# A one-core hybrid decoder layer: the recurrence's first head beside dense columns, another place for the half steps, and a merge with loads and products ahead

## Chip, cores and metric

One core of one Trainium2 chip. The metric is device microseconds of one execution, the median of 3 runs of the kernel before.

## The reference, cut to what matters

One layer of a decoder on 512 prompt tokens and 8 x 4 sample tokens (544 together), width 1024, all in fp32:

```python
x = layer_norm(ALPHA*x + 0.5*(1 + mod[2]) * swiglu(u0, ...), ln_g[0], ln_b[0])
u = x*(1 + mod[4]) + mod[3]
proj = u @ w_in + b_in            # RWKV columns, queries, keys, values, gates, two merge gates
y_a, new_prev, new_wkv = rwkv7_time_mix(p_rw, rw_prev, rw_wkv, ...)
y_b, new_win = nsa_fn(p_q, sigmoid(p_gate), ...)
m = (sigmoid(p_mA) * (y_a @ w_out_a) + sigmoid(p_mB) * (y_b @ w_out_b)) @ w_o
x = layer_norm(ALPHA*x + (1 + mod[5])*m, ln_g[1], ln_b[1])
x = layer_norm(ALPHA*x + 0.5*(1 + mod[8]) * swiglu(u2, ...), ln_g[2], ln_b[2])
```

`rwkv7_time_mix` is, per head of 64: `S = S*w + (S @ -kk)(kk*a)^T + v k^T`, `y = S @ r`; then a group norm over each head's channels, times `ln_w` plus `ln_b`, plus a bonus term, all times `g = sigmoid(gd) @ g2`. `new_prev` is the last token's row of the projected RWKV columns.

## The kernel before, in words

**Products.** A product in fp32 is done as three (`split`, L254 to L265: ScalarE copies the rounded high part `whi`, VectorE subtracts to get `wlo`; then high by high, high by low, low by high). One column of 128 output channels for 544 tokens (a "dense column") is `dense`, 48 matmuls at L280 with 1024 rows of weights, 24 with 512. A "half step" is `dense_half` (L289), 12 matmuls: half of the tokens of one column of `w_out_b`.

**Order of the work.** A tile scheduler orders each engine's instructions by the program's order and priority. Generators (`yield`) interleave independent work: each `next` issues one step. The stages that matter here:

1. The attention's steps, `prompt_steps` (scores at L1125, transposes L1146, values L1163), with one dense column (`dense_todo`) issued after each step, until 5 columns are left; those after step 31, down to 2 (loop at L1456). The last two are issued by the loop behind the loads of `xwa`, `w2e` and others. These columns are merge gates (`merge_gate`), stored to `gdr` in DRAM.
2. The recurrence. There are four `rw_head`s, each two real heads on 128 partitions. `rw_front` loads r, k and v, and in 7 steps computes decay, key norm and the scaled vectors `be`, `ka`, `ar`, `rk` (products at L1541, L1552, L1570, L1575 and by `head_sums` at L1522; transposes of the sample state at L1603). `rw_prompt` and `rw_sample` then run in turn: chunked products L1630, small inverses in blocks of 32 x 32 (four groups of matmuls, L1690, L1698, L1716, L1724), the chunk chain L1783, and for the sample tokens L1820 to L1893. `rw_tail` does the norm, the bonus, the product with `g2t` (L1522 with `sgd`) and the split into `yah`. The next head starts when the one before has taken 9 steps (`RW_LAG`), with up to 4 live. `wob_steps` holds 16 half steps (8 columns of y_b @ w_out_b, times gate, stored as `mbd`); the main loop issues one in every third round at a raised priority. `ar`'s second half (L1589), `ka` (L1593) and `rk` (L1596) are on GpSimd, the rest of the front on VectorE and ScalarE.
3. The merge. The last-token rows are transposed (L1993) and stored, the residual `xT` is read back whole (L2002), and for each of 8 columns the gate and `mbd` are loaded (L2011, L2012), `w_out_a`'s column is loaded and split (L251 raw), 24 matmuls run at L280, VectorE gates and adds, and `ln_affine` (ScalarE, L194) prepares the residual's tile.
4. The product with `w_o`, the norm and the second feed-forward.

PSUM tiles `mm` have two buffers and `sm` the others. Tags `e` (18 buffers) and `f` (17) hold the head's vectors. All loads named here go through SyncE's queue (SP), in its order.

## Time and profile before

| | us |
|---|---|
| median of 3 runs (1776.05 to 1788.5) | 1780.0 |
| the profiled execution | 1790.0 |
| its span | 1788.2 |
| TensorE busy in it | 1683.7 (94%) |
| mean granted TensorE clock | 0.964 |

The profiled execution is 10 us over the median, of which 1.8 lie outside its span. PE is TensorE's matmuls, PEld its weight loads, DVE is VectorE, ACT ScalarE, POOL GpSimd, SP SyncE. A granted clock of 1.00 is 2.4 GHz and 0.50 is 1.2 GHz. Lines such as L280 are lines of the kernel before.

### The profile page before, as it was taken

The page shows a single profiled execution, that of the slowest core. Times are in us where ns is not written, and L with a number is a line of the kernel's source. Part 1 is how long each engine was busy: PE and PEld are TensorE (multiplying, and loading weights), DVE is VectorE, ACT ScalarE, POOL GpSimd, SP SyncE. Part 2 cuts the span into 40 slices and gives each one's busy share as a digit, 9 for nine tenths or more (in the row PEclk, how much of TensorE's full clock was granted, in tenths as well). Part 3 has the DMA queues.
Part 4 walks back from the last instruction along what each step waited for, and adds up shares of the span by engine and source line. Part 5 has one row for each costly group of instructions (what it writes and reads, how often), then busy time and mean ns, then how long its engine had stood idle before and what let it go on. Part 6 is the DMA issues. An engine that isn't in the chain of part 4 may idle for free.

```text
span 1788.2 us, 34732 instructions
## 1 busy us (share of the span) xinstructions
PE 1683.7 (94%) x14710; PEld 1528.2 (85%) x14710; DVE 883.3 (49%) x1820; ACT 601.9 (34%) x1093; POOL 263.3 (15%) x302
## 2 busy tenths in 40 slices
PE   5999999999999999899999979999899999999995
PEld 5888899999998888677787867877798999999994
DVE  6664233223325735555566376775677333333345
ACT  4343221221224543343444242332446321222221
POOL 6640000000000213445200022231002000000001
PEclk9999999999999999999999988898899999999998
DMA  7853653563534285565432051110642323223321
GB/s 274 298 190 113 200 188 95 189 193 114 159 94 88 94 247 159 172 203 156 122 105 85 32 158 51 46 33 21 219 124 71 95 85 94 83 83 95 92 63 51
DMA packets 260725, 224.97 MB, mean 126 GB/s; under 512 B 28741, under 2 KB 225767, under 8 KB 260186
## 3 DMA queue, kind: packets, MB, share of 16 engines
q1 hardware_dynamic: 244946, 182.60, 34.2%
q0 software_dynamic: 9728, 33.56, 5.8%
q10 hardware_dynamic: 5896, 6.60, 1.1%
q8 instruction: 116, 1.90, 0.4%
q14 instruction: 39, 0.32, 0.1%
HBM read 199.55 MB, written 23.17 MB: 125 GB/s over the span
## 4 chain that ended last, share of the span: by engine, by line
PE 78%; DVE 7%; issue 5%; POOL 3%; DMA 3%; ACT 3%; SPq 0%; another core or an unknown queue 0%; ACTq 0%; POOLq 0%; DVEq 0%
PE mm L280 47%; PE mm L289 8%; PE mm L401 5%; PE sm L520 2%; POOL sraw L1217 2%; PE sm L289 2%; PE sm L1820 1%; PE sm L1630 1%; PE mm L1522 1%; PE sm L1658 1%; PE sm L1163 1%; DMA raw<-in_phi_w1t_dram 1%; PE mm L1125 1%; DMA raw<-in_ffn_w_down_dram 1%; DVE e L174 1%
## 5 line engine op out<-in xcount | busy, mean ns | idle before, releaser
L280 PE MATMUL mm<-uh,whi 128*128 128x272 f32 (+1 forms) x1888 | 398.0, 292 | 2.1 <-ACT qs L194 1.3
L280 PE MATMUL mm<-uh,wlo 128*128 128x272 f32 (+1 forms) x1888 | 393.2, 290 | 0.5 <-DVE wlo L180 0.5
L262 ACT CAST whi<-raw 128x1024 fp32r<-128x1024 f32 (+2 forms) x178 | 177.5, 998 | 642.2 <-PE mm L280 582.3
L280 PE MATMUL mm<-ul,whi 128*128 128x272 f32 (+1 forms) x1888 | 392.5, 289 | 0.0
L180 DVE TENSOR_TENSOR wlo<-raw,whi 128x1024 fp32r<-128x1024 f32 (+2 forms) x178 | 208.2, 1170 | 263.7 <-ACT whi L262 257.3
L280 PEld LDWEIGHTS mm<-uh,whi 128*128 128x128 f32 x1888 | 299.0, 189 | 22.2 <-ACT hh L798 9.2
L280 PEld LDWEIGHTS mm<-ul,whi 128*128 128x128 f32 x1888 | 300.4, 189 | 1.0 <-issue 1.0
L280 PEld LDWEIGHTS mm<-uh,wlo 128*128 128x128 f32 x1888 | 298.0, 189 | 1.8 <-DVE sg L174 0.8
L174 DVE TENSOR_TENSOR sg<-mm,sg 128x544 f32<-128x544 f32 (+1 forms) x47 | 32.3, 688 | 165.4 <-PE mm L280 159.2
L677 POOL TENSOR_TENSOR xT<-xT,mr 128x272 f32<-128x272 f32 x24 | 25.2, 1065 | 557.3 <-DVE xT L174 547.8
L401 PE MATMUL mm<-cx,w1h 128*128 128x256 f32 x512 | 100.3, 291 | 3.7 <-ACT cx L353 1.9
L280 PE MATMUL mm<-hh,whi 128*128 128x256 f32 x480 | 99.3, 288 | 0.0
L280 PE MATMUL mm<-hh,wlo 128*128 128x256 f32 x480 | 99.0, 288 | 0.0
L280 PE MATMUL mm<-hlo,whi 128*128 128x256 f32 x480 | 98.9, 287 | 0.0
L401 PEld LDWEIGHTS mm<-cx,w1h 128*128 128x128 f32 x512 | 82.4, 193 | 11.2 <-issue 6.7
L280 PEld LDWEIGHTS mm<-hh,whi 128*128 128x128 f32 x480 | 76.8, 188 | 1.7 <-ACT hh L798 1.7
L280 PEld LDWEIGHTS mm<-hlo,whi 128*128 128x128 f32 x480 | 76.9, 188 | 0.0
L280 PEld LDWEIGHTS mm<-hh,wlo 128*128 128x128 f32 x480 | 76.8, 188 | 0.0
L401 PE MATMUL mm<-cx,w1l 128*128 128x256 f32 x256 | 73.7, 288 | 0.0
L1217 POOL DMA_INDIRECT sraw<-in_cache_kv_sel_dram,idx x64 | 63.6, 993 | 59.5 <-DMA t_new_kv_win_sample_dram<-sraw 22.6
L732 POOL TENSOR_TENSOR yo<-yo,lno 128x512 f32<-128x512 f32 (+1 forms) x5 | 8.4, 1670 | 396.0 <-issue 372.1
L183 DVE SCALAR_TENSOR_TENSOR xT<-mm,modT,xT 128x512 f32<-128x512 f32 (+2 forms) x80 | 46.4, 582 | 40.5 <-PE mm L289 40.5
(530 smaller groups left out, 3006.8 us busy)
## 6 DMA issues: line engine op xcount, KB each, us to landing
araw<-in_w_ada_dram SPq DMA_DIRECT2D x56, 512.0 KB
raw<-in_ffn_w_gate_dram SPq DMA_DIRECT2D x44, 512.0 KB
raw<-in_ffn_w_up_dram SPq DMA_DIRECT2D x44, 512.0 KB
raw<-in_w_in_dram SPq DMA_DIRECT2D x36, 512.0 KB
raw<-in_ffn_w_down_dram SPq DMA_DIRECT2D x32, 448.0 KB
raw<-in_w_ada_dram SPq DMA_DIRECT2D x16, 512.0 KB
raw<-in_ffn_w_down_dram SPq DMA_DIRECT2D x16, 512.0 KB
gdr<-gst ACTq DMA_DIRECT2D x16, 272.0 KB
```

The source lines that it names most:

```text
L174: V.tensor_tensor(out, a, b, ALU.mult)
L180: V.tensor_tensor(out, a, b, ALU.subtract)
L183: V.scalar_tensor_tensor(out, a, s, b, o0, o1)
L262: S.copy(hv, raw)
L280: T.matmul(ps[:m, h, :n], ww[:, k, :m], xx[:, c0:c0 + n], start=(k == 0 and j == 0), stop=(k == nk - 1 and j == 2))
L289: T.matmul(ps[:, :n], ww[:, k, :], xx[:, c0:c0 + n], start=(k == 0 and j == 0), stop=(k == nk - 1 and j == 2))
L401: T.matmul(pss[:, o, 256 * v:256 * v + 256], ww[:, v, o, jj, :], xx, start=(jj == 0 and j == 0), stop=(jj == 7 and j == 2))
L520: T.matmul(hold["ps"][32 * q:32 * q + 32, :], silT[:, k, :], raws_[i][:, h * 512:(h + 1) * 512], start=(k == 0), stop=(k == KT - 1), tile_ ...
L677: G.tensor_tensor(n, n, mr, ALU.subtract)
L1125: T.matmul(ps[:, g, 0:nk], qT[64 * g:64 * g + 64, i, qt * 128:(qt + 1) * 128], kvt[br, 0][64 * g:64 * g + 64, 0:nk], start=True, stop=True)
L1163: T.matmul(acc[64 * g:64 * g + 64, kt * 128:], kvtok[br][:, kt, 128 + 64 * g:192 + 64 * g], pt_[g][:, 512 * kt:384 * kt + 512], start=(br ...
L1217: G.indirect_dma_start(out=t, out_offset=None, in_=seltab, in_offset=bass.IndirectOffsetOnAxis(ap=idx8[:, c * NB + b:c * NB + b + 1], axis=0))
```

## The change

Six edits go together.

1. Three more dense columns are held back in the attention (8 instead of 5 up to step 31, then 5 instead of 2), and the five left are issued one per step beside the first five of the first head's seven front steps. For this the tags that the front needs (`e`, `ar` and others) move to a pool on the right side that opens earlier, and the last gates take their tiles from tag `e`.
2. `rw_prompt` yields True instead of None after each of its first three stages of 32 x 32 blocks, and a half step is issued there instead of in every third round; what is left runs after the last head.
3. `ar`'s second half and `ka` go from GpSimd to VectorE (`rk` stays).
4. The product with `g2t`, the bonus times it, and the affine weight times it move from `rw_tail` to the end of `rw_sample`; the tail has one product fewer and no GpSimd addition.
5. The transposes and stores of the last-token rows move into two of the `wob_steps` (n = 2 and 3).
6. The merge loads three columns ahead, multiplies the first three of four 128-row pieces of the first two columns before their fourth (which needs the last head), reads `xT` tile by tile after each column, and runs `ln_affine` two columns later, the last two inside the product with `w_o`.

```diff
-        if len(dense_todo) > (5 if n < 31 else 2):
+        if len(dense_todo) > (8 if n < 31 else 5):
...
-    for f in dense_todo:
-        f()
     sta.close()
-    stu.close()
-    stw.close()
-    yap = pool("yap")
...
+    stq.close()
+    strp = ExitStack()
+    rp = pool("rp", stack=strp, side="right")
-    NE, NF = 18, 17
+    NE, NF = 18, 14
...
-        G.tensor_tensor(ar[:, 1, :], wc, xr, ALU.mult)
         mul(ar[:, 0, :], wm1, kk)
         mul(be, kk, ta)
         mul(be, be, wi)
-        G.tensor_tensor(ka, km, wi, ALU.mult)
+        mul(ar[:, 1, :], wc, xr)
+        mul(ka, km, wi)
...
-        yield
+        yield True
...
         mul(v272(bon), halves(ps), v272(xv))
-        d["bon"] = bon
+        yield
+        ps = head_sums(g2t[:, ht * 128:(ht + 1) * 128], sgd)
+        gw = ee()
+        act(v272(gw), halves(ps), AF.Identity, scale=pcol(GNW + ht))
+        stt(v272(bon), v272(bon), pcol(GNB + ht), halves(ps), ALU.add, ALU.mult)
+        d.update(bon=bon, gw=gw)
     def rw_tail(ht, d):
...
-        mul(y, y, r2)
-        yield
-        act(y, y, AF.Identity, bias=pcol(GNB + ht), scale=pcol(GNW + ht))
-        G.tensor_tensor(y, y, d["bon"], ALU.add)
-        ps = head_sums(g2t[:, ht * 128:(ht + 1) * 128], sgd)
-        mul(v272(y), v272(y), halves(ps))
-        S.copy(yah[0][:, ht, :], y)
+        mul(gw, gw, r2)
+        yield
+        add(gw, gw, bon)
+        S.copy(yah[0][:, ht, :], gw)
...
     def wob_steps():
         for n in range(KT):
+            if n in (2, 3):
+                for j4 in (2 * n - 4, 2 * n - 3):
...
+    live = [heads.pop(0)]
+    age = {id(live[0]): 7}
+    for _ in range(7):
+        if dense_todo:
+            dense_todo.pop(0)()
+        next(live[0])
+    stu.close()
+    stw.close()
     while heads or live:
...
-        if k % 3 == 1:
-            with tc.high_priority(offset=-WOB_OFF):
-                next(wst, None)
-        k += 1
+            elif said is True:
+                with tc.high_priority(offset=-WOB_OFF):
+                    next(wst, None)
     for _ in wst:
         pass
...
-    SY.dma_start(xT, xsp)
+    def merge_load(n):
+        raw = load_raw(wview(woa, 0, 512, n * 128, (n + 1) * 128))
+        t = [op.tile([128, TOK], F32, tag=tag, name=f"{tag}{n}", bufs=6) for tag in ("gate", "mb")]
+        SY.dma_start(t[0], gdr[0, n])
+        SY.dma_start(t[1], mbd[n])
+        return raw, t
+    ahead = [merge_load(n) for n in range(3)]
+    parts = []
+    for n in range(2):
+        parts.append((mm(), split(ahead[n][0])))
+        merge_part(*parts[n], 0, 3)
     for n in range(KT):
+        if n + 3 < KT:
+            ahead.append(merge_load(n + 3))
+        if n < 2:
+            merge_part(*parts[n], 3, 4)
...
-        ln_affine(0, n)
+        SY.dma_start(xT[:, n, :], xsp[:, n, :])
+        if n > 1:
+            ln_affine(0, n - 2)
     def out_w(n):
+        if n < 2:
+            ln_affine(0, KT - 2 + n)
```

Where the change moves instructions, first on PE (line, operation, out<-in, shape, count), at the end of the first head's front. Before, the last rows of a half step, then the key-norm product, the second head's first products, the state's transposes and the first L1630:

```order
L289 MATMUL sm_1470_10988<-ybh1_10736,whi_1456_10933 128x272
L289 MATMUL sm_1470_10988<-ybh0_10735,wlo_1457_10934 128x272
L1522 MATMUL mm_1459_10951<-e_1453_10926,cst_r_10756 128x272 x2
L1541 MATMUL mm_1516_11191<-w2e_10749,tw_10758 128x128 x4
L1541 MATMUL mm_1516_11191<-w2e_10749,tw_10758 32x128
L1552 MATMUL mm_1523_11230<-xwa_10748,a2t_10750 128x272 x2
L1603 MATMUL sm_1476_11017<-cst_g_118,sraw_1448_10902 128x64 x8
L1630 MATMUL sm_1486_11036<-ar_1473_11006,e_1471_11004 64x128 x8
L1630 MATMUL sm_1487_11047<-ar_1473_11006,e_1471_11004 64x128 x8
```

After (line numbers are three lower), the last rows of the fifth dense column, then the same transposes, the second head's first products and the first L1627:

```order
L279 MATMUL mm_1462_10891<-uh_163_1486,wlo_1453_10814 128x256
L279 MATMUL mm_1462_10891<-uh_163_1486,wlo_1453_10814 128x288
L1600 MATMUL sm_1470_10965<-cst_g_118,sraw_1431_10655 128x64 x8
L1538 MATMUL mm_1505_11129<-w2e_10569,tw_10578 128x128 x4
L1538 MATMUL mm_1505_11129<-w2e_10569,tw_10578 32x128
L1549 MATMUL mm_1512_11168<-xwa_10568,a2t_10570 128x272 x2
L1627 MATMUL sm_1480_10997<-ar_1467_10954,e_1465_10952 64x128 x8
L1627 MATMUL sm_1481_11008<-ar_1467_10954,e_1465_10952 64x128 x8
```

The dense columns, which stood wholly ahead of the front, now end right in front of the transposes; the half step of that place is gone.

PE again, in the blocks of 32 x 32 of the third head. Before, from the second group of blocks (L1698) to the fourth (L1724):

```order
L1698 MATMUL sm_1787_12755<-x32_1762_12595,w1_1775_12667 32x32 x32
L1639 MATMUL sm_1790_12798<-cst_g_118,e_1672_12115 128x128 x4
L1522 MATMUL mm_1803_12857<-e_1674_12122,brk_1802_12855 128x272
L1893 MATMUL sm_1792_12805<-cst_g_118,f_1683_12168 64x128 x4
L1893 MATMUL sm_1793_12811<-cst_g_118,f_1683_12168 64x128 x4
L1783 MATMUL sm_1798_12829<-f_1748_12528,f_1721_12364 64x64 x2
L1522 MATMUL mm_1803_12857<-e_1674_12122,brk_1802_12855 128x272
L1716 MATMUL sm_1800_12835<-t32_1788_12789,f_1691_12198 32x32 x8
L1603 MATMUL sm_1805_12864<-cst_g_118,sraw_1730_12416 128x64 x8
L1783 MATMUL sm_1807_12875<-f_1748_12528,f_1721_12364 64x64 x2
L1716 MATMUL sm_1800_12835<-t32_1788_12789,f_1691_12198 32x32 x8
L1724 MATMUL sm_1808_12879<-x32_1762_12595,w1_1799_12834 32x32 x8
```

After, from the second group (L1695) on, with the product with `g2t` and the transposes of the sample's state:

```order
L1695 MATMUL sm_1786_12719<-x32_1758_12548,w1_1770_12615 32x32 x32
L1636 MATMUL sm_1789_12762<-cst_g_118,e_1671_12084 128x128 x4
L1519 MATMUL mm_1814_12901<-sgd_10581,g2t_10571 128x272
L1890 MATMUL sm_1791_12769<-cst_g_118,s0T_1683_12153 64x128 x4
L1890 MATMUL sm_1792_12775<-cst_g_118,s0T_1683_12153 64x128
L288 MATMUL sm_1793_12783<-ybh0_10555,whi_1781_12682 128x272
L288 MATMUL sm_1793_12783<-ybh1_10556,whi_1781_12682 128x272
```

A half step (12 rows L288) now stands between the second and the third group of blocks, another inside the third group and one ahead of the second; before, one stood ahead of the second and the next behind the fourth, and the stretch above had none.

Last, SP's queue at the end of the recurrence. Before, the last stores (`mbd6`, the states), the whole `xT`, `mbd7`, and the loads of `w_out_a`:

```order
L1962 DMA mbd6_13375<-gst_1856_13180 128x544
L1896 DMA out_new_wkv_sample_dram<-sraw_1890_13438 64x8x64 x2
L1808 DMA out_new_wkv_prompt_dram<-so_1915_13597 64x2x64
L2002 DMA xT2_13825<-xsp_6101 128x4352
L1962 DMA mbd7_13650<-gst_1902_13511 128x544
L251 DMA raw_1948_13843<-in_w_out_a_dram 128x4x128
L251 DMA raw_1952_13883<-in_w_out_a_dram 128x4x128
```

After:

```order
L1978 DMA mbd6_13786<-gst_1942_13752 128x544
L2063 DMA xT2_13838<-xsp_6101 128x544
L1978 DMA mbd7_13825<-gst_1948_13791 128x544
L2063 DMA xT2_13838<-xsp_6101 128x544 x2
L2031 DMA gate0_13852<-gdr0_0_10389 128x544
L250 DMA raw_1955_13850<-in_w_out_a_dram 128x4x128
L2032 DMA mb0_13853<-mbd0_11410 128x544
```

The loads of `w_out_a` and of the gates now stand behind the store `mbd7`, which waits for the last half step, and behind three tiles of `xT` of 272 KB each instead of the whole one.

## Rows read from the trace of the kernel before

**Rows 1.** The page of the profile, two rows: each engine's busy time with its share of the span and its instructions; and PE's granted clock in 40 slices of 44.7 us, in tenths.

```profile
PE 1683.7 (94%) x14710; PEld 1528.2 (85%) x14710; DVE 883.3 (49%) x1820; ACT 601.9 (34%) x1093; POOL 263.3 (15%) x302
...
PEclk9999999999999999999999988898899999999998
```

**Rows 2.** Busy time by stretch (the columns: start and end, length, busy us and instructions of PE, PEld, DVE, ACT, POOL, then PE's granted clock, the busy share of the DMA engines and their rate). The stretches: the end of the attention with its last dense columns; dense columns and the attention's last step; the first head's front; the recurrence; its end with the first two merge columns; the other six merge columns.

```profile
943.60:991.90 48.30, 46.07 (x279) 31.79 (x278) 28.53 (x71) 21.48 (x59) 0.00 (x0) 0.89 0.20 57
991.90:1027.00 35.10, 35.10 (x275) 33.67 (x274) 9.61 (x15) 9.51 (x19) 0.00 (x0) 1.00 0.11 40
1027.00:1048.50 21.50, 11.77 (x79) 9.44 (x78) 12.62 (x18) 13.04 (x27) 5.83 (x4) 0.82 0.95 260
1048.50:1259.00 210.50, 203.12 (x2942) 162.08 (x2943) 144.61 (x384) 62.81 (x124) 47.96 (x51) 0.88 0.18 51
1258.90:1283.30 24.40, 19.43 (x115) 14.97 (x116) 13.42 (x25) 13.75 (x22) 2.68 (x2) 0.72 0.61 196
1283.30:1301.40 18.10, 18.08 (x144) 18.10 (x145) 17.07 (x25) 7.74 (x13) 0.00 (x0) 1.00 0.77 207
```

**Rows 3.** The same columns for pieces of the first of those stretches.

```profile
968.40:979.20 10.80, 8.77 (x53) 5.04 (x52) 9.72 (x23) 7.37 (x20) 0.00 (x0) 1.00 0.07 26
979.20:989.40 10.20, 10.00 (x26) 4.42 (x28) 6.88 (x22) 3.59 (x15) 0.00 (x0) 0.50 0.00 1
```

**Rows 4.** The waits of PE between 943 and 1030 us (who waited at which line, for whom, us in total, times, longest).

```profile
PE mm L1125 <- ACT pp L194: 2.2, 1, 2.2
```

**Rows 5.** The waits of PE between 1027 and 1049 us.

```profile
PE sm L1630 <- DVE e L174: 9.7, 1, 9.7
```

**Rows 6.** The chain of work that ended last, between 1027 and 1050 us (start, us, what).

```profile
1026.93 0.38 PE mm L280 x3
...
1046.47 1.86 DVE e L174
...
1048.46 1.54 PE sm L1630 x14
```

**Rows 7.** VectorE and GpSimd at the end of that front, as a list of instructions (start, us, engine, line, operation).

```profile
1044.06 0.71 DVE L174 TENSOR_TENSOR e<-e,e 128x544 f32<-128x544 f32 x1
1044.69 1.85 DVE L174 TENSOR_TENSOR ar<-e,e 128x544 f32<-128x544 f32 x1
...
1044.08 1.88 POOL L1589 TENSOR_TENSOR ar<-e,e 128x544 f32<-128x544 f32 x1
```

**Rows 8.** The recurrence, cut where PE's granted clock changes; the columns are those of the second group. Of the seven stretches at half clock these are the first, the second, the fifth and the last.

```profile
1048.50:1054.30 5.80, 5.80 (x58) 5.30 (x59) 5.52 (x12) 0.37 (x1) 1.84 (x3) 0.50 0.76 157
...
1081.60:1098.60 17.00, 15.70 (x160) 13.25 (x159) 6.39 (x14) 4.43 (x9) 3.17 (x7) 0.50 0.17 33
...
1194.20:1201.00 6.80, 6.80 (x66) 6.13 (x62) 3.15 (x6) 0.74 (x2) 0.00 (x0) 0.50 0.00 0
...
1235.20:1238.60 3.40, 3.40 (x29) 2.70 (x24) 0.87 (x2) 1.17 (x2) 1.89 (x5) 0.50 0.02 5
```

**Rows 9.** Three us before that fifth stretch and the first three of it, in the same columns; then the costliest groups of matmuls in the three before (line, operation, shapes, count, busy us, mean ns).

```profile
1191.00:1194.00 3.00, 3.00 (x68) 2.61 (x66) 1.42 (x4) 1.32 (x3) 0.79 (x2) 1.00 0.57 93
1194.00:1197.00 3.00, 3.00 (x44) 2.60 (x43) 0.76 (x2) 0.38 (x1) 0.00 (x0) 0.53 0.00 0
...
L1716 PE MATMUL sm<-t,f 32*32 32x32 f32 x28 | 1.2, 192 | 0.0
L1724 PE MATMUL sm<-x,w 32*32 32x32 f32 x22 | 1.1, 193 | 0.0
```

**Rows 10.** The matmuls of one half step alone, in two places (the columns without the other engines).

```profile
1094.50:1097.80 3.30, 3.09 (x12) 2.77 (x12) 0.50 0.02 5
1110.50:1112.70 2.20, 1.78 (x12) 1.56 (x12) 1.00 0.00 0
```

**Rows 11.** PE's work in the recurrence by line, between 1049 and 1259 us: the half steps.

```profile
L289 PE MATMUL sm<-ybh,whi 128*128 128x272 f32 x112 | 28.2, 348 | 0.0
...
L289 PE MATMUL sm<-ybh,wlo 128*128 128x272 f32 x56 | 18.4, 329 | 0.0
```

**Rows 12.** The same between 1258.9 and 1283.3 us: the product with `g2t` and the transposes of `lastc`.

```profile
L1522 PE MATMUL mm<-sgd,g2t 128*128 128x272 f32 x8 | 3.2, 534 | 0.5 <-DVE e L183 0.5
L1993 PE MATMUL sm<-cst_g,lastc 128*9 128x128 f32 x14 | 2.4, 305 | 1.9 <-ACT so L169 1.9
```

**Rows 13.** The chain of work that ended last, between 1255 and 1312 us.

```profile
1249.86 9.23 DMA xT<-xsp
...
1274.77 8.53 PE mm L280 x48
...
1283.32 18.29 PE mm L280 x144
```

**Rows 14.** ScalarE between 1258.9 and 1275 us: the residual's `ln_affine` and the split's first half.

```profile
L194 ACT ACTIVATE xT<-xT,pv 128x512 f32<-128x512 f32 x8 | 6.3, 807 | 1.3 <-DMA xT<-xsp 1.3
...
L262 ACT CAST whi<-raw 128x512 fp32r<-128x512 f32 x2 | 1.2, 602 | 0.0
```

**Rows 15.** Two stretches of 4 us at the end of the recurrence, in the columns of the second group.

```profile
1250.00:1254.00 4.00, 3.45 (x123) 2.90 (x117) 2.80 (x9) 0.00 (x0) 0.00 (x0) 1.00 0.80 274
1254.00:1258.00 4.00, 3.17 (x75) 2.20 (x67) 1.99 (x7) 2.03 (x3) 0.00 (x0) 1.00 0.93 356
```

**Rows 16.** The DMAs issued between 1236 and 1330 us: the sum of their packets.

```profile
DMA packets 20666, 15.86 MB, mean 169 GB/s; under 512 B 1961, under 2 KB 18345, under 8 KB 20530
```

More of the change, by code (lines that the diff above doesn't have):

```diff
@@ L41 @@
 RW_LAG = 9
-RW_SAMPLE = 0
 AHEAD = 2
@@ L1441, in build @@
     dense_cols = [(j * 128, rw_proj, (j,)) for j in (12, 13, 4, 0, 8, 5, 1, 9, 6, 2, 10, 7, 3, 11)]
-    dense_cols += [(MG0 + s_ * D + n * 128, merge_gate, (s_, n, gsp)) for s_ in (1, 0) for n in range(KT)]
+    dense_cols += [(MG0 + s_ * D + n * 128, merge_gate, (s_, n, lambda: gate_tile[0]()))
+                   for s_ in (1, 0) for n in range(KT)]
+    gate_tile = [lambda: gsp.tile([128, TOK], F32, tag="gst", name=nm("gst"), bufs=3)]
     def dense_step(i):
@@ L1934, in rw_head @@
         a, b = rw_prompt(ht, d), rw_sample(ht, d)
-        live, n = [a, b], 0
+        live = [a, b]
         while live:
+            small = False
             for g_ in list(live):
-                if (g_ is a or n >= RW_SAMPLE) and next(g_, live) is live:
+                said = next(g_, live)
+                if said is live:
                     live.remove(g_)
-            n += 1
-            yield
+                else:
+                    small = small or said is True
+            yield small
         yield from rw_tail(ht, d)
@@ L1946, in wob_steps @@
         for n in range(KT):
+            if n in (2, 3):
+                for j4 in (2 * n - 4, 2 * n - 3):
+                    m = min(4, RW_TILES - 4 * j4)
+                    tps = sm()
+                    for j in range(m):
+                        T.transpose(tps[:9, j * 128:(j + 1) * 128], lastc[:, 4 * j4 + j, :], ident)
+                    so = ff([9, 512])
+                    S.copy(so[:, 0:m * 128], tps[:9, 0:m * 128])
+                    cols = slice(512 * j4, 512 * j4 + m * 128)
+                    SY.dma_start(O["new_shift_prompt"][0:1, 0, cols].rearrange("a b -> a b"), so[0:1, 0:m * 128])
+                    SY.dma_start(O["new_shift_sample"][0, :, cols], so[1:9, 0:m * 128])
             raw = wp.tile([128, wn], F32, tag="raw", name=nm("raw"), bufs=4).rearrange("p (a b) -> p a b", a=4)
@@ L1968, in build @@
     heads = [rw_head(ht) for ht in range(4)]
-    live, age, k = [], {}, 0
+    live = [heads.pop(0)]
[6 more added lines that the diff above has]
+    stw.close()
+    yap = pool("yap")
+    yah = [yap.tile([128, 4, TOK], F32R, name=f"yah{i}") for i in range(2)]
+    str_ = ExitStack()
+    wp, wn = pool("wps", stack=str_), 512
+    rq = pool("rq", stack=str_)
     while heads or live:
@@ L1975, in build @@
             age[id(g_)] += 1
-            if next(g_, heads) is heads:
+            said = next(g_, heads)
+            if said is heads:
                 live.remove(g_)
-        if k % 3 == 1:
-            with tc.high_priority(offset=-WOB_OFF):
-                next(wst, None)
-        k += 1
+            elif said is True:
+                with tc.high_priority(offset=-WOB_OFF):
+                    next(wst, None)
     for _ in wst:
@@ L1984, in build @@
     str_.close()
+    strp.close()
     wp, wn = pool("wp2"), 1024
     sty.close()
[L1987 to L1997 removed]
     xp = pool("xp2", stack=stx, side="right")
     xT = xp.tile([128, KT, TOK], F32, name="xT2")
[L2002 removed]
     up = pool("up2")
@@ L2007, in build, with merge_part @@
     u = new_u()
-    gate, mb = {}, {}
-    for n in range(KT):
-        gate[n], mb[n] = [op.tile([128, TOK], F32, tag=tag, name=f"{tag}{n}", bufs=6) for tag in ("gate", "mb")]
-        SY.dma_start(gate[n], gdr[0, n])
-        SY.dma_start(mb[n], mbd[n])
-        ps = mm()
-        raw = load_raw(wview(woa, 0, 512, n * 128, (n + 1) * 128))
-        dense(ps, split(raw), lambda k: (yah[0][:, k, :], yah[1][:, k, :]), 4)
-        ga = gate[n]
+    def merge_load(n):
[4 more added lines that the diff above has]
+        return raw, t
+    def merge_part(ps, w, k0, k1):
+        hv, lv = w
+        for k in range(k0, k1):
+            for j, (ww, xx) in enumerate(((hv, yah[0]), (hv, yah[1]), (lv, yah[0]))):
+                for h in range(2):
+                    T.matmul(ps[:, h, 0:272], ww[:, k, :], xx[:, k, 272 * h:272 * h + 272],
+                             start=(k == 0 and j == 0), stop=(k == 3 and j == 2))
+    ahead = [merge_load(n) for n in range(3)]
[3 more added lines that the diff above has]
+        merge_part(*parts[n], 0, 3)
+    for n in range(KT):
+        if n + 3 < KT:
+            ahead.append(merge_load(n + 3))
+        if n < 2:
+            ps = parts[n][0]
+            merge_part(*parts[n], 3, 4)
+        else:
+            ps = mm()
+            merge_part(ps, split(ahead[n][0]), 0, 4)
+        ga, mb = ahead[n][1]
         stt(v272(ga), v272(ga), 1.0, halves(ps), ALU.add, ALU.mult)
-        add(ga, ga, mb[n])
+        add(ga, ga, mb)
         S.copy(u[0][:, n, :], ga)
         sub(u[1][:, n, :], ga, u[0][:, n, :].bitcast(F32))
-        ln_affine(0, n)
+        SY.dma_start(xT[:, n, :], xsp[:, n, :])
+        if n > 1:
+            ln_affine(0, n - 2)
     def out_w(n):
+        if n < 2:
+            ln_affine(0, KT - 2 + n)
         sl = None if n < 2 else [op.tile([128, 1024], F32R, tag="ow" + c_, name=nm("ow"), bufs=6) for c_ in "hl"]
```

37 lines of the change are left out of this document (12 added, 25 removed).

## The prediction

> **What bounds the kernel now.** I read the page first: TensorE is busy 94% of the span and its granted clock is below full in the slices of the recurrence [rows 1]. So a gain must come from the places where PE idles or runs at half clock. Next, busy time by stretch [rows 2]: the stretch of the first head's front is 21.5 us with 11.77 us of PE work, while the dense columns before it ran without a gap (35.10 of 35.10 us); the recurrence is 210.5 us, PE busy 203.12 at a mean clock of 0.88; its end is 24.4 us with 19.43 busy at 0.72. The waits say who is late: in the front, PE waits once, 9.7 us, for a VectorE product [rows 5], and the chain of work [rows 6] shows that this product ends the front's vector work, 21.2 us after the last dense column (1027.3 to 1048.46). In the recurrence no wait is large: there the clock is the loss.
>
> **The change part by part.** All sums are against the profiled execution, 1790.0 us, which is 10 us above the median; the difference is then taken off the median. A column of 48 matmuls costs 18.29/3 = 6.10 us at full clock [rows 13].
>
> *Attention.* Three columns (18.3 us) leave the attention's steps and keep their cost elsewhere. The stretch that held them is 48.3 us [rows 2], so 30.0 us remain. Of those 10.2 us are already at half clock, behind a dense-free piece in which PE was busy 8.77 of 10.8 us [rows 3], with one wait of 2.2 us for the softmax [rows 4]. After, ten steps stand there without a column instead of seven. The trace doesn't show them so, and I bound this from both sides. Half to full clock is 3.09 to 1.78 us for the same 12 matmuls, 1.74 [rows 10], so a microsecond at half clock loses 0.425. Without loss the 30.0 us would be 30.0 - 10.2 x 0.425 - 2.2 = 23.5; all at half clock, 23.5 x 1.74 = 40.9. So -6.5 to +11. I take one more wait like the one there, +2.5, since the row nearest is a piece of seven such steps that had just one.
>
> *The first head's front.* PE's 11.77 us there hold two half steps, 2 x 1.78 = 3.6 us [rows 10], which move on; 8.2 us of the front's and the second head's products stay. The wait of 9.7 us should go: the front's chain of some 21 us now has five columns, 30.5 us, beside it, and VectorE and ScalarE were each busy under 10 of 35.1 us next to such columns [rows 2]. The two products moved from GpSimd cost VectorE little: such a product took 0.71 us there against 1.88 on GpSimd, and the next one, with GpSimd's beside it all the time, 1.85 [rows 7]. So -9.7 - 3.6 = -13.3. If seven steps at one per column leave a third of the chain uncovered (some 8 us), it is -5; below -14 it can't go, since the wait is then gone.
>
> *The recurrence.* Seven stretches, 5.8 us the first and 3.4 the last, 50.0 us in sum, are at half clock [rows 8]; at 0.425 they lose 21.2 us. Where does the clock fall? The first stretch follows the front's idle time and should go with it. Before the fifth, PE was busy 3.00 of 3.00 us, but 50 of its 68 matmuls were blocks of 32 x 32; in the next three us the granted clock was 0.53 [rows 9]. The change puts 12 matmuls of 128 rows and 272 columns between those groups. I take a third of the half clock (17 us) to remain, between none and all, since it puts a half step behind two of the groups that had none; the saving is 33 x 0.425 = 14.0. Next, 168 matmuls of half steps [rows 11] are 14 half steps; 12 stay, -3.6. The product with `g2t` for the heads that were still in the tail and the transposes of `lastc` come in: 3.2 + 2.4 us at mostly half clock [rows 12], 3.2 us at full. PE idles 7.4 us here now [rows 2]; when it gets faster by 14 us and VectorE has the same 144.6 us and a few products more, its dependencies come late more often: half as much again, +3.7. Sum -10.7, between -20.4 (no half clock left, 1.2 us of new waits) and +3 (none of the clock saved and the waits all the same).
>
> The Trainium skill, page "TensorE: Matmul & The Clock Gate", section "Why this matters for your kernels", says that mid-kernel drops of throughput are avoided by leaving no long idle gaps of PE between bursts of matmuls. The trace differs: in the row named PE had no gap at all and its clock still fell [rows 9]. By that rule the half steps' new place would buy nothing, which is rival 1.
>
> *The end of the recurrence and the first two merge columns.* Before, 24.4 us [rows 2]. PE work there: less the 5.6 us of [rows 12], plus the four half steps that are left, 4 x 1.78 = 7.1, so 20.9 us. The last head's tail is shorter: ScalarE's eight `ln_affine`, 6.3 us [rows 14], and GpSimd's addition stand in it no longer. But SP's queue has the `w_out_a` loads behind the store that waits for the last half step. I put its end about 10 us in (7.1 us of half steps and 3 of the tail's sums). Behind it three tiles of `xT`, `mbd7`, one gate (272 KB each) and one load of 256 KB, 1.65 MB at the 274 to 356 GB/s of [rows 15], are 4.6 to 6.0 us; with the split (0.6 us on ScalarE [rows 14], as much on VectorE) the first matmul starts at 16.6. The 48 matmuls then take 6.1 us, or 8.5 at half clock [rows 13], which I take, since PE idles some 6 us ahead of them: 25.1 us, +0.7. Before, the loads were there early and `xT`, 9.23 us [rows 13], was what the chain waited for. Bounds: -4 (the loads issue while half steps still run) to +5 (a load takes the 9.23 us of `xT`). The other six columns, 18.29 us, stay; so does the entry to `w_o` within 2 us, its two late `ln_affine` being ScalarE work beside PE's products.
>
> Sum: 2.5 - 13.3 - 10.7 + 0.7 = -20.8, 1769.2 for the profiled execution, 1759 on the median.
>
> **The rivals.**
>
> 1. *The clock doesn't follow the half steps.* Then the recurrence gives -3.6 + 3.2 and no new waits, -0.4, and the sum is -10.5: 1769. For: a half step stood ahead of the second group before, too, and seven stretches fell [rows 8]. Against: the falls come behind the blocks, with PE busy [rows 9].
> 2. *The attention's end stays at half clock.* +11 there instead of +2.5: -12.3, 1768. For: the clock fell in just such a piece [rows 3].
> 3. *The front isn't covered.* Its seven steps wait for VectorE behind the columns' splits, and -5 remains of -13.3: -12.5, 1767.5. This is the change not doing what it says. For: the front's last product was late by all of 9.7 us [rows 5].
> 4. *All of the clock comes back*, in the recurrence (21.2 instead of 14.0) and in the first merge columns (2.4): -30.4, 1750.
> 5. *The merge's loads become the bound, and it is slower.* All of them stand behind the last half step: eight columns of 3 x 272 + 256 KB, `mbd7` and the first `w_o` weights are 9.6 MB. They must be there within some 30 us (6.6 to the first matmul, 8.5 and 18.29 for the columns, less the last one), 320 GB/s. At the mean of this part of the program, 169 GB/s [rows 16], they take 57 us: +27, 1786, slower than before. It costs from 320 GB/s down and eats the whole gain at 9.6 MB in 51 us, 189 GB/s. Against: 274 and 356 GB/s where a transfer of `xT` was queued [rows 15]. For: the later columns of the merge now also carry `xT`, which had been there before.
>
> **How the numbers follow.** The forecast has 0.35, rivals 1 to 5 have 0.20, 0.10, 0.10, 0.17 and 0.08. The likeliest is 1759. The range of 1742 to 1779 reaches from rival 4, with 8 us of its own spread, to rivals 1 to 3 with 10 us, and leaves out rival 5 and the double misses. About 1% (17.8 us) is what a measurement of this kernel tells from no change, so 1762 is the border. Below it are seven tenths of the forecast (0.25), nearly all of rival 4 (0.16) and about a fifth of rivals 1 to 3 (0.09): faster 0.50. Rival 5 and a few cases in which two rivals meet are slower, 0.08; the same has 0.42.
>
> **What would show it.** Right: no wait of PE for VectorE at the first L1627 above 1 us; under 20 us of half clock in the recurrence; the first `w_out_a` load issued behind the last half step, with PE idle some 6 us before the merge; the merge's last six columns in 18 to 19 us. Wrong: half clock of 40 us or more in the recurrence (rival 1), 25 us or more of it before the last dense column (rival 2), a wait of several us in the front (rival 3), PE waiting for `raw` in the later merge columns (rival 5).

## The result and the profile after

| | before | after |
|---|---|---|
| median of 15 runs, us | 1784.77 | 1766.95 |
| ratio, 95% interval | | 0.9907 [0.9886, 0.9928] |
| profiled execution: span, us | 1788.2 | 1769.4 |
| PE busy, us | 1683.7 | 1666.9 |
| mean granted clock | 0.964 | 0.974 |

The ratio is 16.6 us of 1784.77, with 12.8 to 20.3 in its interval; the forecast was 20.8 less. The span of the two profiled executions differs by 18.8 us. Where it lies is read from busy time by stretch; this is the changed kernel, cut at the instructions of [rows 2, 3] within 1 us (same columns): the attention's steps without columns; the columns beside the first head's front; the rest of that front; the recurrence; its end with the half steps left and the first two merge columns; the other six; the rest of the program.

```profile
936.30:965.50 29.20, 24.13 (x136) 12.91 (x134) 24.39 (x68) 16.30 (x50) 0.00 (x0) 0.94 0.10 28
965.50:1025.30 59.80, 59.38 (x448) 56.07 (x446) 20.55 (x34) 22.78 (x45) 1.24 (x1) 1.00 0.34 105
1025.30:1028.80 3.50, 3.32 (x25) 2.38 (x24) 3.50 (x4) 2.59 (x6) 2.72 (x4) 1.00 0.51 157
1028.80:1236.20 207.40, 200.81 (x2935) 157.49 (x2935) 142.43 (x392) 68.48 (x135) 32.46 (x40) 0.88 0.19 48
1236.20:1265.80 29.60, 19.58 (x146) 18.31 (x146) 13.69 (x30) 8.23 (x13) 0.00 (x0) 0.77 0.60 192
1265.80:1283.90 18.10, 18.10 (x144) 18.10 (x145) 16.63 (x26) 11.26 (x18) 0.00 (x0) 1.00 0.99 293
1283.90:1769.40 485.50, 457.07 (x3610) 451.99 (x3608) 211.52 (x366) 146.94 (x216) 21.14 (x17) 0.98 0.29 85
```

Attention and front are 92.5 us against 104.9 (48.3 + 35.1 + 21.5 of [rows 2]), the recurrence 207.4 against 210.5 and still at a clock of 0.88, the end 29.6 against 24.4, the six columns 18.1 in both, the rest 485.5 against 486.8. That is -12.4 - 3.1 + 5.2 - 1.3 = -11.6; the other 7.3 us lie ahead of 936.3 us, where the change leaves the order of the matmuls as it was. So the two executions had to be taken again. The kernel before once more, over attention and front, the recurrence and its end:

```profile
944.40:1049.60 105.20, 93.24 (x628) 74.58 (x627) 50.77 (x104) 44.00 (x105) 5.78 (x4) 0.91 0.32 93
1049.60:1260.20 210.60, 203.08 (x2942) 162.07 (x2942) 144.64 (x384) 62.81 (x124) 48.03 (x51) 0.88 0.18 51
1260.20:1284.70 24.50, 19.38 (x116) 14.96 (x116) 13.36 (x24) 13.77 (x22) 2.68 (x2) 0.72 0.61 195
```

and the changed kernel once more, over the same:

```profile
940.80:1033.20 92.40, 86.75 (x604) 71.04 (x602) 48.41 (x105) 41.55 (x101) 3.96 (x4) 0.98 0.27 83
1033.20:1234.60 201.40, 194.84 (x2935) 153.12 (x2935) 141.09 (x392) 68.52 (x136) 32.45 (x40) 0.92 0.19 49
1234.60:1263.20 28.60, 18.63 (x146) 17.42 (x146) 13.67 (x30) 8.19 (x13) 0.00 (x0) 0.82 0.64 206
```

The kernel before repeats itself (105.2, 210.6, 24.5). The changed one repeats attention and front (92.4) and nearly its end (28.6), but its recurrence is now 201.4 at 0.92, with 34 us of half clock (PE at 1.2 GHz, summed over the trace's records of the granted clock) where I had expected 40 to 58. By the means of two and two, attention and front give -12.6, the recurrence -6.1, the end +4.7, and the part ahead, 944.4 and 943.6 us against 940.8 and 936.3, -5.4.

PE's idle time, the span less its busy time, is 104.5 and 104.7 us in the two executions before and 102.5 and 105.3 after. So what the change saved in waits it paid back in other waits, and the gain of the profiles is shorter busy time of PE.

The waits of PE in the changed kernel between 930 and 1330 us:

```profile
PE mm L2040 <- ACT whi L261: 8.9, 1, 8.9
PE mm L1125 <- ACT pp L193: 4.5, 2, 2.6
PE sm L1687 <- DVE t L1671: 2.3, 1, 2.3
...
PE sm L1627 <- DVE e L173: 0.2, 1, 0.2
```

The 9.7 us of [rows 5] are 0.2, the softmax's wait of [rows 4] came twice, the first group of blocks has a new wait of 2.3 us (L1687), and there is one of 8.9 us in front of the merge. The chain of work that ended last shows what that one is (start, us, what):

```profile
1249.32 0.32 SPq L1978
...
1251.26 5.61 DMA raw<-in_w_out_a_dram
1256.88 0.63 ACT whi L261
```

Two neighbouring rows of PE's own list give the wait's two ends:

```profile
1248.40 0.29 PE L288 MATMUL sm<-ybh,wlo 128*128 128x272 f32 x1
1257.55 1.27 PE L2040 MATMUL mm<-yah,whi 128*128 128x272 f32 x4 [8.86 <-ACT whi L261]
```

The last half step's products end at 1248.7; its gating and its store (SPq L1978) stand ahead of the `w_out_a` load, issued at 1251.26 and landed 5.6 us later.

Where the clock falls now, in stretches on either side of two falls in the changed kernel's recurrence (columns as above), and the costliest matmuls ahead of the first fall:

```profile
1101.00:1104.50 3.50, 3.50 (x71) 2.51 (x71) 3.50 (x6) 1.17 (x6) 2.83 (x2) 1.00 0.02 5
1104.50:1108.00 3.50, 3.50 (x14) 2.31 (x14) 3.22 (x5) 0.62 (x1) 0.39 (x1) 0.51 0.01 5
1196.70:1200.10 3.40, 3.40 (x110) 3.06 (x107) 3.37 (x9) 1.22 (x3) 2.85 (x2) 1.00 0.00 0
1200.10:1217.20 17.10, 17.10 (x126) 11.98 (x125) 5.12 (x10) 2.91 (x5) 2.61 (x5) 0.50 0.11 35
...
L1687 PE MATMUL sm<-t,f 32*32 32x32 f32 x64 | 1.9, 192 | 0.0
L1817 PE MATMUL sm<-wide,tk 32*64 32x512 f32 x2 | 1.1, 612 | 0.0
```

PE is without a gap on both sides, as in [rows 9]; the work ahead of both is now the first group of blocks (L1687) and the 32-row products of the sample tokens (L1817), and the second fall lasts 17.1 us although nearly two half steps stand in it.

### The profile page after: what moved, and what is told of

It reads as the page before. It is cut to its first block, busy times and chain, and to the rows that moved or that the text cites. A ratio compares the mean times of both kernels' runs of the same rounds, so it can differ in the third digit from the quotient of the medians.

```text
span 1769.4 us, 34773 instructions
## 1 busy us (share of the span) xinstructions
PE 1666.9 (94%) x14710; PEld 1515.0 (86%) x14710; DVE 879.5 (50%) x1834; ACT 603.1 (34%) x1095; POOL 242.3 (14%) x290
## 4 chain that ended last, share of the span: by engine, by line
PE 79%; DVE 7%; issue 5%; DMA 3%; ACT 3%; POOL 2%; SPq 0%; ACTq 0%; POOLq 0%; DVEq 0%
PE mm L279 45%; PE mm L288 7%; PE mm L400 5%; PE sm L519 2%; PE sm L288 2%; PE sm L1817 1%; PE mm L2040 1%; PE mm L1519 1%; POOL sraw L1217 1%; PE sm L1163 1%; PE sm L1655 1%; DMA raw<-in_phi_w1t_dram 1%; PE sm L1627 1%; PE mm L1125 1%; DVE xT L173 1%
## 5 line engine op out<-in xcount | busy, mean ns | idle before, releaser
L738 DVE TENSOR_TENSOR rtmp<-mm,modT 128x32 f32<-128x32 f32 x32 | 6.1, 192 | 117.0 <-PE mm L279 117.0
```

## Experiments

Each is timed beside the kernel before. The mean half-clock time is that of a whole execution, worked out from the granted clock listed for every timed run, 2 x (1 - clock) x span; it counts idle PE too. The batches of the kernel before have 115 to 121 us of it. A figure of half clock for one stretch is of the one profile of that kernel.

| kernel | runs | ratio, 95% interval | mean us at half clock |
|---|---|---|---|
| the changed kernel | 15 | 0.9907 [0.9886, 0.9928] | 82 |
| e1_old_place | 5 | 0.9884 [0.9867, 0.9902] | 79 |
| e2_four_halves | 6 | 0.9918 [0.9898, 0.9937] | 99 |
| e3_dense_back | 6 | 0.9915 [0.9894, 0.9936] | 86 |
| e4_old_merge | 6 | 0.9902 [0.9881, 0.9922] | 81 |
| e5_late_pool | 6 | 0.9905 [0.9883, 0.9927] | 80 |
| e6_no_halves | 12 | 0.9964 [0.9950, 0.9978] | 110 |
| e7_old_tail | 6 | 0.9903 [0.9874, 0.9932] | 87 |
| e8_gpsimd_muls | 8 | 0.9941 [0.9916, 0.9966] | 97 |
| e9_other_queue | 6 | 0.9886 [0.9858, 0.9914] | 81 |
| e10_front_free | 12 | 1.0051 [1.0030, 1.0071] | 120 |

From here on the recurrence ends at the last head's state transposes (L1798), 1.9 us behind the cut of the tables above. On that cut the recurrence of the changed kernel and its end with two merge columns are, in its first and its second profile:

```profile
1028.80:1238.10 209.30, 201.72 (x2947) 158.12 (x2949) 144.25 (x396) 68.70 (x135) 32.46 (x40) 0.88 0.19 47
1238.10:1265.80 27.70, 18.68 (x138) 17.68 (x136) 11.87 (x25) 8.02 (x12) 0.00 (x0) 0.76 0.64 205
...
1033.20:1236.50 203.30, 195.69 (x2949) 153.70 (x2951) 142.91 (x396) 68.78 (x136) 32.45 (x40) 0.92 0.19 49
1236.50:1263.20 26.70, 17.78 (x138) 16.84 (x135) 11.86 (x25) 7.92 (x12) 0.00 (x0) 0.81 0.68 220
```

**The half steps back in every third round** (from the changed kernel).

```diff
-            elif said is True:
-                with tc.high_priority(offset=-WOB_OFF):
-                    next(wst, None)
+        if k % 3 == 1:
+            with tc.high_priority(offset=-WOB_OFF):
+                next(wst, None)
+        k += 1
```

> The changed kernel with the half steps back in every third round of the main loop; all 16 then end before the last head's end. Theory A (the clock in the recurrence does not follow the half steps' place, since the changed kernel's trace still has 48.2 us at half clock there against 50.2 before): half clock of 40 to 58 us here too, the recurrence 4 to 8 us longer because four more half steps (7 us) stand in it, and the stretch from its end to the third merge column shorter by 4 to 8 us than the 27.65 us of the changed kernel, because no load waits for a last half step; total within 5 us of the changed kernel, ratio 0.989 to 0.993. Theory B (the new place does spare clock and the one trace hides it by chance): half clock over 58 us, the total 8 us or more above the changed kernel, ratio 0.995 or more.

Ratio 0.9884, the lowest of all. The recurrence with all 16 half steps, and its end with two merge columns:

```profile
1031.80:1243.90 212.10, 207.45 (x2993) 165.26 (x2993) 148.97 (x401) 69.43 (x136) 36.05 (x40) 0.90 0.18 48
1243.90:1262.10 18.20, 11.45 (x89) 9.99 (x88) 9.45 (x19) 10.16 (x15) 0.00 (x0) 0.81 0.90 277
```

```profile
PE mm L2041 <- ACT whi L261: 4.5, 1, 4.5
```

212.1 us, 2.8 and 8.8 over the changed kernel's two profiles with four half steps (7.1 us) more in it; half clock 44.4 us; the end 18.2 instead of 27.7 and 26.7, and the wait for the first weights 4.5 instead of 8.9. Theory A held in kind: the half clock is within its range, while the end gained more than its 4 to 8 us and the ratio is just below its 0.989. The place of the half steps among the blocks is not what spares clock; and leaving four of them for the end costs.

**A fourth half step per head, ahead of the first group of blocks.**

```diff
         S.copy(av[:, :, :, 1, :], ps.rearrange("p (c h i) -> p c h i", c=4, h=2))
-        yield
+        yield True
```

> The changed kernel with one more half step per head, issued ahead of the first group of 32 x 32 blocks, where the clock fell in the changed kernel's trace (1050, 1104 and 1200 us); none is left for the end. The first merge loads then wait for no half step: theory M says PE's wait of 8.9 us for the first w_out_a weights goes to under 4 us, and the stretch from the recurrence's end to the third merge column falls from 27.65 to 19 to 22 us. Four half steps (7 us) go into the recurrence, so without any help of the clock the sum is about even (ratio 0.988 to 0.992); if the half step ahead of the first group holds the clock (theory B), half clock in the recurrence falls from 48 to under 30 us and the ratio is 0.983 to 0.987.

```profile
1033.90:1251.50 217.60, 212.87 (x2997) 171.22 (x2999) 143.43 (x400) 74.38 (x143) 34.14 (x40) 0.87 0.21 58
1251.50:1271.70 20.20, 14.08 (x90) 11.62 (x86) 11.69 (x23) 5.58 (x9) 0.00 (x0) 0.66 0.59 184
```

```profile
PE mm L2040 <- ACT whi L261: 2.0, 1, 2.0
```

Theory M held: the wait is 2.0 us and the end 20.2. Theory B fell: although the fourth half step stood exactly at the falls, half clock in the recurrence was 58.0 us in this profile, and that of the whole execution 99 over the runs, against 82 in the changed kernel.

**The dense columns back, and then the pool back as well.** In e3 the thresholds are 5 and 2 again and the columns left run ahead of the first head's seven steps; in e5 the front's tiles besides come from a pool on the left that opens behind the attention's pools.

```diff
-        if len(dense_todo) > (8 if n < 31 else 5):
+        if len(dense_todo) > (5 if n < 31 else 2):
...
+    for f in dense_todo:
+        f()
     for _ in range(7):
-        if dense_todo:
-            dense_todo.pop(0)()
         next(live[0])
```

> The changed kernel with its dense columns back: three in the attention's steps, two ahead of the first head's front, none beside it. If the front's cover is what the change gained, PE's wait for VectorE in front of the first L1627 comes back with 8 to 11 us, the part from the attention's end to the first L1627 grows from 94.3 to 104 to 108 us, and the total is 10 to 14 us above the changed kernel, ratio 0.996 to 1.000. If the gain lies elsewhere, ratio 0.991 to 0.994.

> The changed kernel with the dense columns back and the front's tiles in a pool that opens behind the attention's pools, as before, so that the front's loads wait for the last column. Theory F1 (the early pool gives back some 3 us, the columns beside the front some 7): PE's wait in front of the first L1627 is 9 to 11 us against 6.8 in the run with the columns back alone, and the ratio is 0.992 to 0.996. F2 (the front's tiles and loads being early plays no part): wait 6 to 8 us, ratio within 0.002 of that run's 0.9915.

The waits of PE at the first L1627, in e3 and (two lines higher in the code) in e5:

```profile
PE sm L1627 <- DVE ar L173: 6.8, 1, 6.8
```

```profile
PE sm L1625 <- DVE ar L173: 6.8, 1, 6.8
```

In both 6.8 us come back of the 9.7, less than the 8 to 11 expected of e3, whose ratio is that of "the gain lies elsewhere". Of e5's theories F2 held: when the tiles are to be had plays no part. Attention and front in e3, then in e5:

```profile
938.90:1033.80 94.90, 85.67 (x603) 70.18 (x603) 48.62 (x104) 43.04 (x104) 3.82 (x4) 0.97 0.34 101
...
941.60:1041.10 99.50, 90.32 (x606) 72.15 (x605) 49.67 (x105) 43.20 (x104) 3.81 (x4) 0.92 0.33 99
```

e3 takes 94.9 us, 2.5 over the changed kernel: the wait of 6.8 less the softmax's second wait (2.3, which is gone here) and less half clock, none of it here while PE works, against 3.4 us. e5 takes 99.5, 7 over it, with 10 us of half clock while PE works. At equal clock both come to some 4 us for the columns beside the front; whether the clock of this part goes with the columns is taken up below. The ratios differ by 0.0008 and -0.0002 from the changed kernel's, inside their intervals.

**The second half of `ar` and `ka` on GpSimd again**, on top of e3.

```diff
-        mul(ar[:, 1, :], wc, xr)
-        mul(ka, km, wi)
+        G.tensor_tensor(ar[:, 1, :], wc, xr, ALU.mult)
+        G.tensor_tensor(ka, km, wi, ALU.mult)
```

> The changed kernel with the dense columns back and, besides, the second half of ar and ka on GpSimd again. With the columns back alone PE waited 6.8 us at the first L1627, with or without the early pool, against 9.7 in the kernel before. Theory V (the two products on VectorE instead of GpSimd took the 2.9 us from the front's chain): the wait is 9 to 10.5 us here, and the ratio 0.992 to 0.995. Rival (they play no part): 6 to 7.5 us and 0.990 to 0.993. If GpSimd's products beside VectorE's were what cost clock in the recurrence, the mean half clock rises from 86 us to over 105.

```profile
PE sm L1627 <- DVE e L173: 7.3, 1, 7.3
```

7.3 us, as the rival had it: these products account for 0.5 of the 2.9 us. The ratio is 0.9941, in theory V's range, with 97 us at half clock against e3's 86 (the 105 named were not reached). The 10 us more of half clock would be 4.5 us if PE is busy in them, about the whole difference between the two ratios, but the interval overlaps that of e3.

**The kernel before with no half step in the first head's front.**

```diff
-        if k % 3 == 1:
+        if k % 3 == 1 and k > 6:
```

> The kernel before with one edit: no half step is issued in the first seven rounds of the recurrence, so that the two that stood between the first head's front products go to later rounds; all 16 still end before the last head does. With the dense columns back, the late pool and GpSimd's products, the variants of the changed kernel still have that part of the program 5 us shorter than the kernel before at equal clock. Theory H (the two half steps delayed the front's own chain): from the last dense column to the first L1630 it takes 15.5 to 18 us against 21.3, PE's wait there falls from 9.7 to 7 to 8.5 us, and since the two half steps then stand in the recurrence the ratio is 0.996 to 0.999. Rival (they filled PE's idle time and cost nothing): 20 to 22 us, the wait longer by their 3.6 us, 12 to 14 us, ratio 1.000 to 1.003. If the missing half steps between the front's products are also what gives the clock back, the mean half clock falls from 118 to under 100 us and the ratio to 0.990 to 0.994.

From the last dense column to the first L1630, and the merge's last six columns; then the waits:

```profile
1020.80:1040.30 19.50, 10.15 (x52) 7.34 (x50) 10.93 (x19) 12.25 (x26) 5.71 (x3) 0.76 1.03 266
...
1276.50:1299.90 23.40, 20.04 (x146) 19.61 (x145) 16.55 (x25) 8.35 (x13) 0.00 (x0) 0.93 0.66 196
```

```profile
PE mm L280 <- ACT whi L262: 10.1, 2, 6.9
PE sm L1630 <- DVE e L174: 8.6, 1, 8.6
```

19.5 us against 21.3, the wait 8.6: between the two theories. The half steps' 3.6 us did not all come back, as the front's products L1570 show, in the kernel before and in e10:

```profile
1031.44 1.89 PE L1570 MATMUL sm<-cst_r,sig 128*128 128x256 f32 x8
...
1024.11 3.63 PE L1570 MATMUL sm<-cst_r,sig 128*128 128x256 f32 x8 [0.78 <-DVE sig L186]
```

Without a half step ahead of them they waited 0.8 us for VectorE and then took 3.63 us instead of 1.89, at half clock. The whole is slower, 1.0051, at the other end: the last half step comes later and SP's loads stand behind it. `xT` is issued 1.4 us ahead of the recurrence's end (1253.0 against 1254.4) instead of 11.0 (1249.9 against 1260.9), and the last six merge columns take 23.4 us instead of 18.1. The waits are put down to the split of `w_out_a`; of the first, 6.9 us, the chain of work runs through the last head's own split (`yah`), so that only the second, 3.3 us among the six columns, is the loads'. The clock did not come back (120 us).

**No half step in the recurrence.**

```diff
             elif said is True:
-                with tc.high_priority(offset=-WOB_OFF):
-                    next(wst, None)
+                pass
```

> The changed kernel without any half step in the recurrence; all 16 run behind the last head (28.5 us at full clock), 12 of them more than in the changed kernel. Theory A (half steps among the blocks don't set the clock): half clock in the recurrence 38 to 60 us, the recurrence 18 to 22 us shorter, the end 20 to 23 us longer, ratio 0.990 to 0.994. Theory B (they hold the clock up, if not enough): over 65 us at half clock in the recurrence, which is then only 8 to 15 us shorter, ratio 0.995 to 1.000.

```profile
1034.30:1223.70 189.40, 178.79 (x2789) 139.53 (x2791) 134.75 (x378) 63.52 (x125) 35.08 (x40) 0.85 0.12 27
1223.70:1277.40 53.70, 39.36 (x295) 37.91 (x294) 20.17 (x43) 15.81 (x25) 0.00 (x0) 0.84 0.68 218
```

The recurrence is 189.4 us, 19.9 under the changed kernel's first profile and 13.9 under its second, the end 53.7. Neither theory held whole: this one profile has 58.0 us at half clock in the recurrence, theory A's side, while the twelve runs have 110 us in the whole execution against 82, and their ratio of 0.9964 lies outside A's range. So with no half step in the recurrence an execution has some 28 us more of half clock, wherever the half steps had stood. That it lies in the recurrence is likely but not shown: the 58.0 us are barely above the 28 to 56 of the five profiles compared below. PE also idles more there, 10.6 us against 7.6, so that the half steps had filled idle time as well.

**The merge as before**, in the changed kernel: `xT` whole, one column's loads after another, `ln_affine` at once.

```diff
-    ahead = [merge_load(n) for n in range(3)]
...
+    SY.dma_start(xT, xsp)
     for n in range(KT):
...
+        dense(ps, split(raw), lambda k: (yah[0][:, k, :], yah[1][:, k, :]), 4)
...
+        ln_affine(0, n)
```

> The changed kernel with the merge as before (whole xT first, one column's loads after another, no products ahead, ln_affine at once). Theory M (the merge starts late because its loads stand behind the last half step's store, whatever the merge's own order): PE still waits 6 to 12 us for the first w_out_a weights, and the total is 0 to 6 us above the changed kernel, ratio 0.991 to 0.995. Rival (the new order of loads, gates and tiles of xT in between, is what delays it): the wait falls under 4 us and the ratio is 0.986 to 0.989.

```profile
PE mm L279 <- ACT whi L261: 13.4, 1, 13.4
```

```profile
1235.40:1265.90 30.50, 17.06 (x137) 16.30 (x137) 13.04 (x27) 11.37 (x17) 0.00 (x0) 0.78 0.73 252
```

The wait is 13.4 us, the end 30.5 against 27.7 and 26.7. Theory M held in kind, its wait beyond the 12 it allowed and its ratio just below its range: the loads ahead are worth 3 to 4 us in these profiles, and the order of merge and loads is not what made the merge late. The ratio, 0.9902, is the changed kernel's.

**The tail as before**: the product with `g2t`, the bonus and the affine in each head's tail again.

```diff
-        ps = head_sums(g2t[:, ht * 128:(ht + 1) * 128], sgd)
-        gw = ee()
...
+        d["bon"] = bon
...
+        act(y, y, AF.Identity, bias=pcol(GNB + ht), scale=pcol(GNW + ht))
+        G.tensor_tensor(y, y, d["bon"], ALU.add)
+        ps = head_sums(g2t[:, ht * 128:(ht + 1) * 128], sgd)
```

> The changed kernel with the tail as before: the product with g2t, GpSimd's addition of the bonus and the affine stand in each head's tail again. All runs of the changed kernel and its variants with half steps in the recurrence have 79 to 99 us at half clock over their timed executions, the kernel before 115 to 118. Theory T (the product with g2t, two matmuls of 272 columns per head that moved from the tails into the recurrence, is what gives clock back): the mean half clock rises from 81 to over 100 us and the ratio is 0.996 to 1.000. Rival (it plays no part; the tail's chain is hidden behind the half steps that are left): half clock 75 to 92 us, ratio 0.990 to 0.994.

The rival held: ratio 0.9903, half clock 87 us. Its recurrence's end, 28.6 us, is within 2 us of the changed kernel's 27.7 and 26.7:

```profile
1237.20:1265.80 28.60, 19.35 (x141) 18.14 (x140) 11.55 (x24) 9.66 (x14) 2.67 (x2) 0.82 0.65 211
```

**The first weights from another queue**, on top of e1.

```diff
-        raw = load_raw(wview(woa, 0, 512, n * 128, (n + 1) * 128))
+        raw = load_raw(wview(woa, 0, 512, n * 128, (n + 1) * 128), G if n < 3 else None)
```

> The half steps in every third round again (the fastest variant so far, ratio 0.9884), and the first three loads of w_out_a issued from GpSimd's queue instead of SP's, where they stood behind five tiles of xT and two stores. Theory M (the order on SP is what holds the first weights): PE's wait for them falls from 4.5 to under 2 us, the stretch from the recurrence's end to the third merge column from 18.2 to 14 to 16.5 us, ratio 0.986 to 0.988. Rival (the loads are held by the memory that the recurrence's tiles give free, or by the traffic of xT): the wait stays at 4 us or more, ratio 0.988 to 0.990.

```profile
PE mm L2041 <- ACT whi L261: 4.4, 1, 4.4
```

The chain of work that ended last there, between 1236 and 1256 us:

```profile
1239.30 6.91 DMA xT<-xsp
...
1246.24 0.81 ACT xT L193
...
1247.65 0.70 ACT xT L193
...
1248.90 0.71 ACT xT L193
1249.61 0.52 ACT whi L261
```

The rival's numbers, 4.4 us and 0.9886, but not quite its reason. The first load was issued 0.3 us behind the last half step instead of 4.2 us in e1; what is late now is ScalarE's half of the split (`whi`), which stands in ScalarE's order behind three `ln_affine` of `xT`, and these wait for `xT`'s DMA of 6.9 us: the same chain as in [rows 13], one step on. The end is 21.9 us, longer than e1's 18.2.

No variant beats the changed kernel beyond both intervals; e1_old_place is the fastest measured, 1764.75 against 1766.95 us, and keeps the simpler rule for the half steps.

## Why the prediction was right or wrong

The total came out in size and sign, 16.6 us for 20.8, but in part by luck. By the two pairs of profiles the recurrence fell 4.6 us short of its term and the end 4.0; what filled the gap was 5.4 us in the part ahead of the change, for which the prediction had no term, and 1.8 us more than forecast in attention and front.

*The attention's steps (+2.5).* The steps without columns took 29.2 us where 32.5 were forecast. The wait came as forecast, 4.5 us in two for 2.2 in one, but half clock did not stay at the 10.2 us I carried over: 3.4 in both profiles of the changed kernel. While PE works, attention and front have 3 to 7 us of half clock in all eight profiles with the columns held back, and about 10 us in five of the six with the attention's old order; the sixth (e3) has none. So the columns' new place may well spare clock here, but e3 speaks against it, and it is not settled.

*The front (-13.3).* With the attention -10.8, measured -12.4 and -12.8 (profile by profile). The wait of 9.7 us went to 0.2; 2.3 us of waiting came back at the first group of blocks (L1687), besides the softmax's second wait. My reason was the larger part of it: putting the columns back returns 6.8 us. Of the rest 1.1 us go with the half steps ahead of the front's products (e10), 0.5 us with GpSimd's products (e8), and none with the early tiles (e5); about 1 us has no name.

*The recurrence (-10.7).* This is where the prediction failed: the step "I take a third of the half clock (17 us) to remain". Measured are 48 and 34 us in the changed kernel's two profiles, and 56, 34 and 28 in e3, e4 and e5, whose edits leave the recurrence alone: 40 us on average, where I had put the sign of being wrong. The term of -14.0 is (50 - 40) x 0.425, about -4. The +3.7 for new waits did not come either: PE idled 6.6 us in both profiles, against 7.4 before. What I read from [rows 9], that the clock falls behind blocks of 32 x 32 with PE busy, was right as far as it went; but the falls moved to the next such stretch, the first group of blocks and the sample's 32-row products, and with half steps in any other place (e1) the half clock is the same. The Trainium skill's rule ("TensorE: Matmul & The Clock Gate", section "Why this matters for your kernels": no idle gaps) does not name these falls either, since PE has no gap in them. Rival 1 had the mechanism, in that the clock does not follow the half steps' place; by the number, -6.1 by the means of the profiles, its -0.4 was no nearer than my -10.7.

*The end and the merge (+0.7).* Measured +5.2 and +4.1. The mechanism was as forecast (the loads behind the last half step's store, PE idle, the columns then at half clock), the size was not: I put the last half step's end at 10 us and the first matmul at 16.6; the last products ended at 12.5 (1248.7 less 1236.2), their store was issued at 13.1, and the first matmul came at 21.3. The half steps ran between the last head's sums and not at once, and the issue of four DMAs took another 2 us. Without half steps left (e1, e2) the end is 18.2 and 20.2 us, against 27.7 and 26.7.

*What made up for it.* By the runs' clocks, half clock fell from some 118 to 82 us, 36 x 0.425 = 15 us if PE is busy in it, nearly the whole gain. The profiles agree: half clock while PE was busy is 98 and 100 us before, 68 and 56 after, and 37 x 0.425 = 16 of the 19 us by which PE's busy time fell. I had looked for it in the recurrence; by the pairs of profiles 14 us of it lie ahead of the change, 15 in attention and front (8 of these idle time of PE, which is worth nothing), about 9 in the recurrence and 4 to 8 behind the merge. No single part taken back restores the 118: not the half steps' place, the columns, the pool, the tail, the merge (79 to 87 us); GpSimd's products with the columns back go a third of the way from e3's 86 (97), no half steps at all three quarters (110). Several parts taken back together were not tried, nor the moved transposes and stores (edit 5) or the smaller count of `f` buffers. The part ahead of the change, whose matmuls are the same in the same order, had 23.9 us at half clock twice before and 10.2 twice after; e10, which up to the first head's front is the kernel before, had 10.2 there too, and the changed kernel's variants 6.8 to 17.1. So these 14 us, worth 5 to 6 of the profiles' 20 us, look like a draw of the execution, though no run gives the clock of that part over many executions. The cause of the larger part of the gain is not settled: it is the clock, and not a part of the change that I can name.

Rival 5 did not come: behind the first weights the six columns ran without a wait at 293 GB/s (against 207 before). Rivals 2 and 3 did not either, and rival 4 in no execution.

## What to carry to other kernels

When work is moved off a crowded stage, look at what the last piece of it now stands in front of: four half steps left for the end held a queue, and with them the end was 8.5 to 9.5 us longer than without (e1), for 7.1 us of work that they took off the recurrence. A stage whose clock falls gives different times in different executions of the same kernel, so a term that rests on it is a distribution: take two profiles before crediting a change with it. When a wait is freed, follow the chain one step on before the next edit (the weights' queue was freed, and ScalarE's order held them as long).

## What the runs showed of the hardware

- A recurrence that no edit touched had 28 to 56 us at half clock in five profiles, while that of the kernel before had 50.2 and 50.4 in two.
- PE without any idle time dropped to 1.2 GHz and stayed there for 17.1 us, with 126 matmuls at work, 23 of them of two half steps (128 rows, 272 columns).
- A VectorE product of 128 x 544 beside GpSimd's took 1.85 us instead of 0.71 [rows 7], and still moving two of them off GpSimd shortened the front's chain by only 0.5 us.
